# First loads of a two-block transformer kernel: smaller pieces in another order, and zero matmuls on TensorE ahead of the first GEMM

## The chip, the core and the metric

The kernel runs on one core of a Trainium2 chip. The metric is the device time of one execution in microseconds; a run has several executions, and the median is quoted. One further execution is recorded by the hardware profiler, and every row below comes from that one.

## The reference, cut to what matters

Two transformer blocks run one after the other on 256 tokens of width 1024, all in float32. What the change touches is the very beginning: the RMS norm and the first product of block one.

```python
h = _rmsnorm(x, g_mix[l])              # x: 256 x 1024
z = h @ w_in[l]                        # w_in: 1024 x 5632; q is columns 2048 to 3071
x_rnn, g_rnn, q, k, v, gate_a, gate_b = jnp.split(z, SPLIT_IDX, axis=-1)
...                                    # RG-LRU branch, sliding window attention, gates, w_out
x = x + jnp.square(jax.nn.relu(hm @ w_up[l])) @ w_down[l]
...                                    # gated embedding; then block two: latent attention, pooling,
                                       # memory attention, and a mixture of 32 experts, top 2
return rms_norm(h, final_norm_g)
```

The norm's factor is a number per token, so the kernel multiplies the raw x by the gain g_mix first, runs the product, and applies the factor to the result.

## The kernel before, in words

**Products.** TensorE multiplies in float32 by a split: each operand is written as a high part in the fast float32 format plus the rest, and a product is three matmuls, high by high (L313), low by high (L314) and high by low (L315). `split` (L278) makes the parts: ScalarE casts the high part (L279), VectorE subtracts it from the source (L280). This is done for the activations (tile `st`) and for every weight (tile `raw` into `w`).

**The first GEMM.** `gemm` (L317) takes two halves of the tokens (t = 0, 1), 512 output columns, and eight blocks of 128 rows of the weight (k = 0 to 7). The weight comes in raw tiles of four blocks (1 MB each), and each raw tile is split and used in *parts* of two blocks. So the first GEMM (the first 512 columns of q) is four parts of 12 matmuls each: part 0 has k = 0 and 1, part 1 has k = 2 and 3 (both from the first raw tile), parts 2 and 3 have k = 4 to 7 (from the second raw tile).

**The order.** `run` (L242) writes the program part by part. Ahead of a part it splits weights ahead: before part 0 the weights of parts 0 and 1; before part 1 those of parts 2 and 3; from then on always two parts ahead (L257: `ahead <= done + min(self.LEAD, done + 1)`, with LEAD = 2). A callback in `after_split[1]` runs between the split of part 0's weights and that of part 1's. After a part's matmuls the work that was put off with `later(n, fn)` comes due: `later(0)` after the first part, `later(1)` after the second, and so on. Then the background generators ("lanes") each go one step, or two while fewer than FAST = 18 parts are done (L272). From the beginning to `self.region.close` (due after the fourth part) the order on every engine is as written (`manual_schedule`); what is written later is ordered by a planner that may also put it into earlier gaps, until a second region in written order before the experts (L1054). The engines take their instructions strictly in the order they were given.

**The start.** `setup` (L498) loads the first quarter of x, loads two row tiles of small parameters, builds the identity, and turns the first of the row tiles into columns (gain vectors). `start` (L613) transposes x in quarters of 256 KB, (c, t) being the columns c·512 to c·512+511 of token half t: four transposes (L286), then a multiply by the gain on VectorE (L290, tile `xg`), then a split into `st`. Quarter (0,0) is transposed in `start`, quarter (0,1) in the callback, the quarters (1,0) and (1,1), which are k = 4 to 7, after part 0. `factor` computes the norm's factor after part 1. The loads on the queue of SyncE (SP) are: x (0,0); weight blocks k = 0, 1 (512 KB); x (0,1); weight blocks k = 2, 3 (512 KB); x (1,0); x (1,1); then raw tiles of 1 MB. The first four stand in `rawload` (L300).

**Later.** `background` lanes carry the attention (`swa_q`, `swa_k`) and the recurrence; `self.step(lambda: self.until(swa))` (L685) empties the attention lanes before the product that needs them. The experts at the end stream their weights from memory.

Of the kernel before, what the change touches and what calls it, by code (L numbers as in the profile page):

```python
# [12 lines left out]
BF16 = mybir.dt.bfloat16  # L13
# [8 lines left out]
P = 128  # L22
# [77 lines left out]
class Net:  # L100
# [199 lines left out]
    def rawload(self, w, k0, nk, c0, n):  # L300
        src = w[k0 * P:(k0 + nk) * P, c0:c0 + n].rearrange("(k p) n -> p k n", p=P)
        if not self.raws:
            def first(tile):
                self.nc.sync.dma_start(tile[:, 0:2, 0:n], src[:, 0:2])
                self.load_x(0, 1)
                self.nc.sync.dma_start(tile[:, 2:4, 0:n], src[:, 2:4])
                self.load_x(1, 0, 1)
            return Raw(first)
        return Raw(lambda tile: self.nc.sync.dma_start(tile[:, 0:nk, 0:n], src))
# [7 lines left out]
    def gemm(self, st, KT, w, c0, n, evac):  # L317

        accs = {}
        for k0 in range(0, KT, 4):  # L320
            nk4 = min(4, KT - k0)
            r = self.rawload(w, k0, nk4, c0, n)
            for q in range(0, nk4, 2):
                nk = min(2, nk4 - q)
                def fn(h, l, k=k0 + q, nk=nk):
# [172 lines left out]
    def setup(self):  # L498
        nc, a, cp = self.nc, self.a, self.cp
# [6 lines left out]
        nc.vector.memset(warm, 0.0)  # L506
        nc.scalar.activation(warm, warm, AF.Tanh)
        self.ident = cp.tile([P, P], F32, name="ident")
        make_identity(nc, self.ident)
# [7 lines left out]
        turn(0, 0, _SPLIT_ROW)  # L517
        self.later(1, lambda: turn(1, _SPLIT_ROW, N_ROW - _SPLIT_ROW))

    def load_x(self, c, *ts):  # L520
# [92 lines left out]
    def start(self):  # L613

        nc, st = self.nc, self.st0
        g = self.col("g_mix")
        part = lambda c, t: self.X[t][:, c * 512:(c + 1) * 512]
        x0 = self.trans_gain(part(0, 0), 0, 4, g)
        def first():
            self.split(x0, st.v(0, 0, 0, 4), st.v(1, 0, 0, 4))  # L620
            self.trans_split([(1, part(0, 1))], st, 0, 4, g)
        self.after_split[1] = first
        def factor():
# [6 lines left out]
            for t in range(2):  # L630
                st.r[t], st.rh[t] = r[:, t:t + 1], rh[:, t:t + 1]
        self.later(0, lambda: self.trans_split([(t, part(1, t)) for t in range(2)], st, 4, 4, g))
        self.later(1, factor)
        self.later(3, self.region.close)
        def more():
            self.setup1()
            self.lanes.insert(0, self.setup_steps())
        self.later(3, more)

# [1135 lines left out]
```

## Time and profile before

| | |
|---|---|
| median of 3 runs | 972.24 us (971.6 to 977.51) |
| the profiled execution | 971.25 us |
| its span, first to last instruction | 969.5 us |
| PE busy (matmuls) | 900.0 us, 93% of the span |
| DVE busy | 547.4 us, 56% |
| ACT busy | 472.6 us, 49% |
| moved by DMA | 222.65 MB |

The span is 1.75 us shorter than the time of the same execution; the rest lies before the first and after the last recorded instruction. PE is TensorE, PEld its weight loads, DVE VectorE, ACT ScalarE, POOL GpSimd, SP the engine that issues most DMAs; a "q" behind a name is the engine's sequencer, which issues DMAs and waits. All times in rows are microseconds from the start of the span. An arrow "<-" in brackets names what ended an engine's wait.

### The profile page before, as it was taken

How to read it: one execution, taken by the hardware profiler on the slowest of the kernel's cores; microseconds unless marked ns; L12 is line 12 of the kernel's file. 1: busy time of each engine (PE TensorE's matmuls, PEld its weight loads, DVE VectorE, ACT ScalarE, POOL GpSimd, SP SyncE). 2: the span in 40 equal slices, each digit the busy share in tenths (PEclk: the TensorE clock that was granted, in tenths of full speed). 3: DMA queues.
4: the chain of work that ended last, by engine and by line, in shares of the span. 5: the costliest groups of instructions: out<-in, count | busy, mean ns of one | idle time of the engine just before them, and what ended most of it. 6: DMA issues, size and time to landing. Idle time of an engine off the chain costs nothing.

```text
span 969.5 us, 14260 instructions
## 1 busy us (share of the span) xinstructions
PE 900.0 (93%) x5265; PEld 697.7 (72%) x5265; DVE 547.4 (56%) x1101; ACT 472.6 (49%) x900; POOL 34.6 (4%) x71
## 2 busy tenths in 40 slices
PE   6999999999999999999999999999989999647775
PEld 5889898888999999988888887998864444213112
DVE  5986889776675555577765568755455221101002
ACT  5666789654664544456666635545432323002002
POOL 4200000000000000000200000000000000000000
PEclk9999999999999999999999999999998999779868
DMA  9644235495375555544854544454848999999994
GB/s 292 217 153 153 88 131 177 140 321 176 108 247 185 202 178 190 178 145 145 259 180 153 188 150 161 164 184 138 307 166 322 403 405 406 402 406 410 375 408 174
DMA packets 97784, 222.65 MB, mean 230 GB/s; under 512 B 9378, under 2 KB 13739, under 8 KB 96427
## 3 DMA queue, kind: packets, MB, share of 16 engines
q1 hardware_dynamic: 94016, 218.91, 63.5%
q10 hardware_dynamic: 3691, 2.74, 0.9%
q8 instruction: 44, 0.72, 0.3%
q14 instruction: 33, 0.27, 0.1%
HBM read 220.59 MB, written 1.05 MB: 229 GB/s over the span
## 4 chain that ended last, share of the span: by engine, by line
PE 80%; DMA 13%; DVE 3%; issue 1%; ACT 1%; POOL 0%; SPq 0%; DVEq 0%; ACTq 0%; POOLq 0%
PE acc L313 18%; PE acc L315 18%; PE acc L314 17%; DMA raw<-in_w_exp_up_dram 6%; PE pt L1540 5%; PE pt L314 3%; PE pt L315 3%; PE pt L313 3%; DMA rawa<-in_w_exp_down_dram 3%; PE pt L1562 2%; PE pt L1490 1%; DMA rawa<-in_w_exp_up_dram 1%; PE pt L286 1%; DMA raw<-in_w_exp_gate_dram 1%; PE acc L1571 1%
## 5 line engine op out<-in xcount | busy, mean ns | idle before, releaser
L280 DVE TENSOR_TENSOR w<-raw,w 128x512 fp32r<-128x512 f32 (+4 forms) x288 | 273.6, 969 | 115.6 <-ACT w L279 113.6
L279 ACT CAST w<-raw 128x512 fp32r<-128x512 f32 (+4 forms) x288 | 236.3, 847 | 153.9 <-PE acc L315 117.0
L313 PE MATMUL acc<-w,st 128*128 128x512 f32 (+2 forms) x508 | 197.2, 392 | 0.0
L314 PE MATMUL acc<-w,st 128*128 128x512 f32 (+2 forms) x508 | 196.9, 388 | 0.0
L315 PE MATMUL acc<-w,st 128*128 128x512 f32 (+2 forms) x508 | 192.9, 388 | 0.2 <-DVE w L280 0.2
L1540 PE MATMUL pt<-raw,xg 128*32 128x512 f32 (+1 forms) x360 | 95.7, 669 | 40.3 <-DMA raw<-in_w_exp_up_dram 40.3
L315 PEld LDWEIGHTS acc<-w,st 128*128 128x128 f32 x508 | 95.5, 188 | 18.9 <-DVE w L280 0.6
L313 PEld LDWEIGHTS acc<-w,st 128*128 128x128 f32 x508 | 95.8, 189 | 18.4 <-ACT st L279 0.5
L314 PEld LDWEIGHTS acc<-w,st 128*128 128x128 f32 x508 | 95.7, 189 | 17.4 <-DVE st L280 0.2
L1540 PEld LDWEIGHTS pt<-raw,xg 128*32 128x32 f32 (+1 forms) x360 | 22.1, 126 | 95.1 <-issue 91.4
L280 DVE TENSOR_TENSOR y<-pt,y 128x512 fp32r<-128x512 f32 x20 | 13.8, 692 | 129.3 <-ACT y L279 129.3
L314 PE MATMUL pt<-st,w 128*128 128x256 f32 x256 | 72.4, 283 | 1.9 <-DVE w L280 1.9
L315 PE MATMUL acc<-st,w 128*128 128x256 f32 x256 | 73.7, 288 | 0.0
L313 PE MATMUL acc<-st,w 128*128 128x256 f32 x256 | 73.5, 287 | 0.0
L314 PE MATMUL acc<-st,w 128*128 128x256 f32 x256 | 73.4, 287 | 0.0
L313 PE MATMUL pt<-st,w 128*128 128x256 f32 x256 | 72.3, 283 | 0.0
L315 PE MATMUL pt<-st,w 128*128 128x256 f32 x256 | 71.8, 283 | 0.0
L1556 ACT COPY hT<-pt 128x256 f32<-128x256 f32 x10 | 3.7, 373 | 97.4 <-PE pt L1554 97.4
L314 PEld LDWEIGHTS pt<-st,w 128*128 128x128 f32 x256 | 49.1, 192 | 2.3 <-DVE w L280 2.1
L313 PE MATMUL acc<-w,hid 128*128 128x512 f32 x128 | 50.0, 390 | 0.0
L314 PE MATMUL acc<-w,hid 128*128 128x512 f32 x128 | 49.9, 390 | 0.0
L315 PE MATMUL acc<-w,hid 128*128 128x512 f32 x128 | 49.8, 389 | 0.0
(393 smaller groups left out, 1391.0 us busy)
## 6 DMA issues: line engine op xcount, KB each, us to landing
raw<-in_w_in_dram SPq DMA_DIRECT2D x31, 1024.0 KB, 5.3
raw<-in_w_exp_gate_dram SPq DMA_DIRECT2D x45, 512.0 KB, 9.5
raw<-in_w_exp_up_dram SPq DMA_DIRECT2D x45, 512.0 KB, 10.2
rawa<-in_w_exp_down_dram SPq DMA_DIRECT2D x44, 512.0 KB, 9.1
raw<-in_w_up_dram SPq DMA_DIRECT2D x16, 1024.0 KB, 5.7
raw<-in_w_down_dram SPq DMA_DIRECT2D x16, 1024.0 KB, 6.2
raw<-in_w_exp_down_dram SPq DMA_DIRECT2D x10, 1024.0 KB, 11.0
rawa<-in_w_exp_gate_dram SPq DMA_DIRECT2D x38, 256.0 KB, 7.8
```

Source lines behind the costliest of these rows:

```text
L279: self.nc.scalar.copy(h, src)
L280: self.nc.vector.tensor_sub(l, src, h.bitcast(F32))
L286: self.nc.tensor.transpose(p[:, i, :], src[:, i * P:(i + 1) * P], self.ident)
L313: mm(acc, xh, wh, start=start, stop=False)
L314: mm(acc, xl, wh, start=False, stop=False)
L315: mm(acc, xh, wl, start=False, stop=stop)
L1490: nc.tensor.matmul(p, xs[t][i][:, k * P:(k + 1) * P], oh[b, t], start=n == 0, stop=n == 3)
L1540: nc.tensor.matmul(guP[p][q].rearrange("s (j f) -> s j f", j=2), xg[b, hf][:, k, j * P + q.start:j * P + q.stop], gu_of(x, k), start=kt == ...
L1556: nc.scalar.copy(hT[p], q)
L1562: nc.tensor.matmul(q[s], hT[p][:, f, s], d_of(x, f, c), start=f == 0, stop=f == 1)
L1571: nc.tensor.matmul(acc[t, c], stt[b][:, j, t, :], y[p, c][i], start=False, stop=p == NP - 1 and i == 1)
```

## The change

The first raw tile is cut into parts of one, one and two blocks instead of two and two, so that the first GEMM has five parts. Its loads are cut in the same way, and x (0,1) is issued between the first and the second block. Both quarters (0,0) and (0,1) are now transposed in `start`, and the callback only splits them. A bf16 tile of zeros is set on VectorE, and TensorE multiplies it by itself into a PSUM tile that nobody reads: six matmuls of 512 columns in `setup`, one after the first group of transposes and four after the second. What was put off to after the first, second and fourth part is put off by one part more; the second row tile's transpose (`later(1)` in `setup`) is not.

```diff
@@ rawload, first raw tile
-                self.nc.sync.dma_start(tile[:, 0:2, 0:n], src[:, 0:2])
+                self.nc.sync.dma_start(tile[:, 0:1, 0:n], src[:, 0:1])
                 self.load_x(0, 1)
+                self.nc.sync.dma_start(tile[:, 1:2, 0:n], src[:, 1:2])
                 self.nc.sync.dma_start(tile[:, 2:4, 0:n], src[:, 2:4])
                 self.load_x(1, 0, 1)
@@ gemm
+            cuts = [0, 1, 2, 4] if not self.raws else [*range(0, nk4, 2), nk4]
             r = self.rawload(w, k0, nk4, c0, n)
-            for q in range(0, nk4, 2):
-                nk = min(2, nk4 - q)
+            for q, nk in zip(cuts, (b - a for a, b in zip(cuts, cuts[1:]))):
@@ setup
         nc.scalar.activation(warm, warm, AF.Tanh)
+        self.zeros = self.act([P, 512], BF16, name="zeros")
+        nc.vector.memset(self.zeros, 0.0)
+        self.unused = self.pt()
+        self.keep(6)
@@
+    def keep(self, n):
+        for _ in range(n):
+            self.nc.tensor.matmul(self.unused, self.zeros[:, 0:P], self.zeros, start=True, stop=True)
@@ start
-        x0 = self.trans_gain(part(0, 0), 0, 4, g)
+        xs = []
+        for t in range(2):
+            xs.append(self.trans_gain(part(0, t), 0, 4, g))
+            self.keep(1 + 3 * t)
         def first():
-            self.split(x0, st.v(0, 0, 0, 4), st.v(1, 0, 0, 4))
-            self.trans_split([(1, part(0, 1))], st, 0, 4, g)
+            for t in range(2):
+                self.split(xs[t], st.v(0, 0, t, 4), st.v(1, 0, t, 4))
...
-        self.later(0, lambda: self.trans_split([(t, part(1, t)) for t in range(2)], st, 4, 4, g))
-        self.later(1, factor)
-        self.later(3, self.region.close)
+        self.later(1, lambda: self.trans_split([(t, part(1, t)) for t in range(2)], st, 4, 4, g))
+        self.later(2, factor)
+        self.later(4, self.region.close)
...
-        self.later(3, more)
+        self.later(4, more)
```

## Rows read from the trace of the kernel before

**Rows 1.** The page: busy time by engine, and the chain that ended last by engine.
```profile
PE 900.0 (93%) x5265; PEld 697.7 (72%) x5265; DVE 547.4 (56%) x1101; ACT 472.6 (49%) x900; POOL 34.6 (4%) x71
PE 80%; DMA 13%; DVE 3%; issue 1%; ACT 1%; POOL 0%; SPq 0%; DVEq 0%; ACTq 0%; POOLq 0%
```

**Rows 2.** Waits, whole span: who waited for whom, total us, times, longest.
```profile
PE pt L1540 <- DMA raw<-in_w_exp_up_dram: 40.3, 16, 10.2
PE pt L286 <- DMA x<-in_x_dram: 3.9, 1, 3.9
...
PE pt L1321 <- DVE sel L1318: 2.6, 1, 2.6
...
SPq L1445 <- DVE w L280: 18.7, 3, 9.0
```

**Rows 3.** Chain of waits, 0 to 60 us: start, length, what.
```profile
1.75 6.84 DMA x<-in_x_dram
8.63 1.12 PE pt L286 x4
9.75 0.43 PE acc L313
...
13.35 0.23 PE acc L315
13.59 0.45 PE pt L286 x4
...
14.79 0.63 ACT st L279 x2
...
15.91 1.06 ACT w L279
16.99 1.24 DVE w L280
18.27 0.50 PE acc L315
```

**Rows 4.** Timeline, 0 to 20 us: start, length, engine, line, what.
```profile
0.89 0.06 DVE L506 MEMSET s<- 128x1 f32 x1 [0.89 <-PEq L1759]
1.27 0.43 SPq L304 DMA_DIRECT2D raw<-in_w_in_dram  x1
3.51 0.38 PE L515 MATMUL pt<-ident,rows 88*128 88x88 f32 x1 [3.51 <-DMA rows<-in_rows_dram]
4.80 0.69 DVE L290 TENSOR_TENSOR xg<-pt,cols 128x512 f32<-128x512 f32 x1 [0.24 <-PE pt L286]
5.31 0.33 SPq L523 DMA_DIRECT2D x<-in_x_dram  x1
5.68 0.69 SPq L309 DMA_DIRECT2D raw<-in_w_in_dram  x1
7.86 0.68 DVE L280 TENSOR_TENSOR st<-xg,st 128x512 fp32r<-128x512 f32 x1
19.27 0.20 DVE L516 COPY cols<-pt 128x49 f32<-128x49 f32 x1
```

**Rows 5.** First DMAs, issue to landing: L304, L523 (four issues), then the 1 MB tile.
```profile
DMA to landing us min/median/max: 4.3/4.3/4.3
...
DMA to landing us min/median/max: 2.8/6.8/7.3
...
raw<-in_w_in_dram SPq DMA_DIRECT2D x1, 1024.0 KB, 8.6
```

**Rows 6.** Windows: stretch, length, busy by engine (count), PEclk, DMA share, GB/s.
```profile
5.00:8.00 3.00, 0.00 (x0) 0.00 (x0) 1.78 (x3) 1.56 (x2) 0.00 (x0) 1.00 0.84 202
8.00:11.00 3.00, 2.37 (x8) 2.08 (x9) 1.23 (x2) 0.49 (x1) 1.62 (x9) 1.00 1.06 393
...
150.00:160.00 10.00, 10.00 (x49) 8.34 (x49) 9.85 (x16) 9.76 (x23) 0.00 (x0) 1.00 0.48 156
```

**Rows 7.** Line 848, the attention lanes' last product: idle time before it.
```profile
  ACT r L727: 2.4, 2
```

## The prediction

> **What bounds the kernel now.** I read the page first. The reader is to see that PE is busy 93% of the span and carries 80% of the chain, and that DMA carries most of the rest [rows 1]. The list of waits says where PE stands still: 40.3 us before the experts' products, for their weights, 3.9 us for x and 3.51 us for the parameter rows at the very start, and elsewhere in pieces of 2.6 us and less [rows 2, 4]. So from the first GEMM to the experts PE is a queue with hardly a gap, and a microsecond won or lost in the first 19 us arrives at the end as a microsecond. The experts' part is bound by DMA, but the load queue there waits for buffers that VectorE's splits set free (L1445 waits for L280, 18.7 us [rows 2]), and these follow PE, so it shifts along.
>
> Then the chain of the first stretch, which is the one that the change touches [rows 3]. It goes: x (0,1) lands 6.84 us after its issue at 1.75; its transposes; part 0's twelve matmuls, the first ones at 0.43 us each and the last at 0.23; transposes of k = 4 to 7; VectorE's gain multiply; ScalarE's cast of x; then ScalarE's cast and VectorE's subtraction of the weights of part 2, and its third matmul, which starts at 18.27 and, 0.50 later, ends at 18.77. From there PE runs without a gap. That end, 18.77, is the number to beat: it is matmul 27 of the GEMM. The granted clock's column shows 1.00 all along [rows 6], but 0.43 us for 512 columns is the level of 1.2 GHz and 0.23 that of 2.4, so the first half dozen matmuls run at the lower one.
>
> **The change, part by part.** *Zero matmuls in setup.* VectorE sets the zeros right after its first memset, which it did at 0.89 [rows 4], so PE can start at some 1.3 us. Six matmuls at 0.43 are 2.6 us and end near 4.0. The first row transpose stood at 3.51 [rows 4]: it and the first x transposes come 0.5 us later, and the gain multiply, 4.80 to 5.49 before [rows 4], ends near 6.0. Nobody needs it before the second quarter.
>
> *Order of the loads.* x (0,1) now has 512 KB ahead of it on SP's queue instead of 768. The weight piece that had that place landed 4.3 us after its issue at 1.27, at 5.6 [rows 4, 5]. So x (0,1) lands at 5.6 instead of 8.6; the bounds are these two, and I take 5.6 because the bytes ahead are the same. Block k = 1 gets the old place of x (0,1), 8.6. Four transposes (1.12) and a gain multiply (0.69) bring the second quarter to 7.4. The five further zero matmuls on PE cost 0.43 and 1.7 us at the lower clock, up to 8.4; they are hidden, because VectorE is later than that: its subtractions now queue behind the second multiply, w (half the size, 0.68) to 8.1, x (0,0) to 8.8, x (0,1) to 9.5, and w of k = 1 to 10.2 [rows 4].
>
> *First matmuls.* The first can start at 8.4, the second at 8.8, and the twelve of parts 0 and 1 end near 11.3 if the clock is up (12 by 0.23 is 2.8 us); before, twelve had ended at 13.6 [rows 3]. That is 2.3 us won, of which 6 by 0.20, 1.2 us, is the clock. If this came through, the kernel would be 2.3 us faster.
>
> *What is late next.* Behind part 1 stand the transposes of k = 4 to 7. Quarter (1,1) is loaded by the last of four issues that took 6.8 to 7.3 us [rows 5], the last issued at 5.31 [rows 4]: it is there between 12.1 and 12.6, whatever PE does. So PE waits, transposes until 13.1 (0.45), and runs part 2 (k = 2, 3; 2.8 us) to 15.8. In itself that is still fine.
>
> *The moved step.* The x work for k = 4 to 7 was due after part 0, ahead of the split of the second raw tile. Now it is due after part 1; and before part 1 `run` splits two parts ahead, which are k = 2, 3 and k = 4, 5. The weights k = 4, 5 are in the second raw tile. So on ScalarE and VectorE, which keep the written order here, the x work now stands **behind a weight split that waits for the second raw tile**. That tile was issued at 5.68 [rows 4] and landed 8.6 us later [rows 5], at 14.3. The sum from there: ScalarE's cast 1.06, to 15.4; VectorE's subtraction 1.24, to 16.6; the second row tile's copy, which is now also due here, 0.20 [rows 4], to 16.8; gain multiply 0.69, to 17.5; ScalarE's cast of x 0.63, to 18.1; VectorE's second multiply ends then too; its subtraction 0.68, to 18.8. Then the second and third matmul of k = 4 end at 19.1 and 19.35. Before it was 18.77. **The head is 0.6 us longer, not 2.3 shorter**: the gain is spent in PE's wait for k = 4 to 7, from 15.8 to 18.
>
> Bounds for the unknown landing of the second raw tile: its bytes ahead are the same, so I take 14.3. Earlier: from 5 to 8 us DMA moved 202 GB/s, from 8 to 11 us 393 [rows 6]; if the new order closed that, 1.46 us (3 by 191/393), the head would be 0.9 us shorter. Later: one load more stands in the queue. 256 KB took 2.8 us and 512 KB 4.3 [rows 5], so two halves one after the other cost 2 by 2.8 less 4.3, 1.3 us more: the head would be 1.9 us longer. I take no extra, because DMA overlaps several loads and is full from 8 us on, at a share of 1.06 [rows 6].
>
> The Trainium skill speaks against the cut: its page "DMA: Bandwidth & Descriptors", section Bandwidth, tells one to batch transfers to a megabyte or more, and its anatomy section gives each DMA (on the path issued by GpSimd) a fixed part of about 2.0 us beside its bytes. By that figure, as an estimate, one piece more would cost up to 2.0 us if nothing overlapped, and the sum would be near 974.8. The trace agrees that a piece has a fixed part (half the bytes took 2.8 us, not 2.15 [rows 5]), but not that the parts add up while other loads are under way.
>
> *The rest.* One part more before the eighteenth means that the lanes make one step fewer while they step twice. It costs nothing as long as they are empty when `until` asks; see the second rival. The profiled execution would come to 971.25 + 0.6 = 971.9; the median of the runs stands 1.0 us above that execution, so I say 972.24 + 0.6 = **972.8**.
>
> **Rivals.** *A: the gain comes through.* The second raw tile and quarter (1,1) land early enough, or x's casts are ordered ahead of the waiting weight split. For it: DMA has room between 5 and 8 us. Against: the bytes and the written order. Time: 972.24 − 2.3 = 969.9.
>
> *B: slower, by the attention lanes.* They lose a step, and the last product of attention (L848) is emitted in the drain ahead of the product that needs it. ScalarE and VectorE are almost full there (9.76 and 9.85 of 10 us [rows 6]), so a late step is not caught up. That line has PE and its weight loads waiting 2.4 us in all for ScalarE already [rows 7]; as much again gives 972.8 + 2.4 = 975.2. It decides if the lanes are not empty when `until` is reached. Against: over the span they are busy 56 and 49% [rows 1], so the planner has room elsewhere.
>
> *C: the zeros don't lift the clock.* Then the first twelve matmuls end at 12.5 instead of 11.3, still no later than quarter (1,1) lands: 972.8 again, and A shrinks to 971.1. The trace before has no matmul of zeros, so nothing decides it; transposes alone, at 8.63, did not spare the first matmuls the 0.43 [rows 3]. It lies across the others; 1 in 5.
>
> **How the numbers follow.** Forecast (head −0.9 to +1.9) 0.47, A 0.27, B 0.19, and 0.07 for a planner that orders the later work otherwise by over 1% of the time, 9.7 us, which is about what a measurement can tell from no change. For that much PE has no gaps ahead of the experts to win, and to lose it a whole stage would have to fall out of step: 0.03 faster, 0.04 slower. The range goes from A with a microsecond of spread (968.8) to B with the late bound (974.1 + 2.4) and a microsecond (977.5): the median of three also moves, one run before was at 977.51. All three named cases lie within 1%: 0.93.
>
> **What would show it.** In the changed kernel's trace: x (0,1)'s transposes near 6 us; twelve matmuls done by 11 to 12.5; the first real matmuls at 0.23 (A, forecast) or 0.43 (C); VectorE idle before the subtraction of k = 4, 5 for ScalarE, and ScalarE for the second raw tile's DMA, near 14.3; PE idle for VectorE's `st` or `xg` near 16 to 18; matmul 27 ending near 19.35. If it ends at 17 or less the step on the moved work is wrong. B would show as a longer wait at L848 near 170 us. If the difference of the two times isn't that of matmul 27, the carry-through is wrong.

## The result, and the profile after

The changed kernel takes 986.0 us (median of 4 runs, 984.92 to 986.32), beside 971.92 for the kernel before (4 runs, 971.36 to 977.51): a ratio of 1.0136, with a 95% interval of 1.0115 to 1.0156. (The ratios here and below are estimated from all the runs, and need not be the quotients of the two medians.) It is 14 us slower; 972.8 was forecast, and the range ended at 977.5. The profiled execution took 985.95 us, with a span of 984.3; before it was 971.25 and 969.5. The difference of the spans, 14.8 us, is what has to be found. Lines below the edit have moved: L313 to L315 are now L314 to L316, L726 is L740, L727 is L741, L848 is L862.

First the page, busy time by engine and the chain by engine, as in [rows 1].

```profile
PE 910.6 (93%) x5276; PEld 700.6 (71%) x5276; DVE 546.5 (56%) x1103; ACT 473.1 (48%) x901; POOL 35.9 (4%) x71
PE 79%; DMA 14%; DVE 3%; ACT 2%; issue 1%; SPq 0%; POOL 0%; ACTq 0%; DVEq 0%; POOLq 0%
```

The shares tell nothing: PE is busy 10.6 us longer, with 11 instructions more, the eleven zero matmuls. A busy PE can be a slow PE. VectorE and ScalarE are busy for as long as before, to within a microsecond. Nor does the list of waits over the whole span show it: the experts' wait for their weights is 40.4 us, as it was [rows 2].

```profile
PE pt L1554 <- DMA raw<-in_w_exp_up_dram: 40.4, 16, 10.0
```

So I looked for landmarks: the same instruction in both traces. Two do it: the first eviction of the branch gates (ScalarE), and the first multiply that takes the attention's projection (VectorE, tile `gate`). Timeline of the kernel before (columns: start, length, engine, line, what):

```profile
69.57 1.86 ACT L430 ACTIVATE gate<-acc,s 128x512 f32<-128x512 f32 x3
...
181.40 1.28 DVE L414 SCALAR_TENSOR_TENSOR gate<-gate,acc 128x512 f32<-128x512 f32 x2
```

The same two in the changed kernel:

```profile
71.51 1.85 ACT L431 ACTIVATE gate<-acc,s 128x512 f32<-128x512 f32 x3
...
195.60 0.68 DVE L415 SCALAR_TENSOR_TENSOR gate<-gate,acc 128x512 f32<-128x512 f32 x1
```

At the first the changed kernel is 1.9 us behind, at the second 14.2, at the end 14.8. So between these two executions the head makes 1.9 us, and **12.3 us are lost between 70 and 196 us**, in a stretch that the change does not touch. The head isn't the same in every execution, as the part on the prediction shows; the 12.3 are counted from landmark to landmark and don't hang on it.

**The head.** The chain of waits from 0 to 60 us, which answers to [rows 3] (start, length, what):

```profile
5.64 3.78 DMA x<-in_x_dram
9.44 0.75 DVE w L280
10.19 0.67 DVE st L280
10.90 0.79 PE acc L315
...
15.53 0.43 PE acc L316
15.96 0.27 PE pt L520
16.23 1.06 PE pt L286 x8
17.30 0.23 PE acc L314
```

Its first line is a later quarter of x; the profile infers that link, and VectorE stood in its multiply for x (0,1) until 9.5. From the second on, the matmuls of parts 0 and 1 follow each other at 0.43 us, from 10.90 to 15.96, in spite of the zeros. The timeline shows how that came (it answers to [rows 4]; what is in brackets is the idle time before, and who ended it):

```profile
1.30 2.74 PE L529 MATMUL pt<-zeros 128*128 128x512 bf16 x6 [1.30 <-DVE zeros L510]
...
8.14 0.66 PE L286 MATMUL pt<-ident,x 128*128 128x128 f32 x4 [2.67 <-DMA x<-in_x_dram]
8.31 8.05 SPq L310 DMA_DIRECT2D raw<-in_w_in_dram  x4
...
8.63 1.09 PE L529 MATMUL pt<-zeros 128*128 128x512 bf16 x4
...
14.41 1.05 ACT L279 CAST w<-raw 128x1024 fp32r<-128x1024 f32 x1 [2.76 <-DMA raw<-in_w_in_dram]
...
15.49 1.23 DVE L280 TENSOR_TENSOR w<-raw,w 128x1024 fp32r<-128x1024 f32 x1 [2.13 <-ACT w L279]
...
16.63 0.20 DVE L521 COPY cols<-pt 128x49 f32<-128x49 f32 x1
16.90 1.29 DVE L290 TENSOR_TENSOR xg<-pt,cols 128x512 f32<-128x512 f32 x2
17.62 1.22 ACT L279 CAST st<-xg 128x512 fp32r<-128x512 f32 x2 [2.17 <-DVE xg L290]
```

After the six zeros and the first transposes PE waits 2.67 us for x (0,1), which lands at 8.14. The second transposes run fast (4 in 0.66, where [rows 3] has 1.12), and so do the four zeros (1.09 for 4). Then the clock falls, as the windows show (stretch, length, PE, PEld, DVE, ACT and POOL busy, PEclk, DMA share, GB/s):

```profile
5.00:9.00 4.00, 1.33 (x8) 0.68 (x7) 0.86 (x2) 1.24 (x2) 0.59 (x4) 1.00 0.90 284
9.00:9.50 0.50, 0.50 (x5) 0.29 (x2) 0.50 (x2) 0.00 (x0) 0.41 (x3) 0.96 0.97 340
9.50:16.00 6.50, 5.75 (x14) 3.58 (x12) 4.37 (x7) 3.13 (x4) 6.50 (x16) 0.50 1.03 364
```

In the landings (least, median, most), which answer to [rows 5], the first 256 KB of weights took 3.7 us and the slowest quarter of x, (0,1), 6.4:

```profile
DMA to landing us min/median/max: 3.7/3.7/3.7
...
DMA to landing us min/median/max: 2.8/6.1/6.4
```

This is one execution. The same beginning ran again in e1, e9, e10, e11, e13 and e14 below. There too PE waits 2.84 to 2.90 us for x (0,1), but the transposes behind the wait take between 0.66 and 1.12 us, fewer matmuls run at 0.43 us, and the twelfth ends between 14.1 and 15.2 us.

**The stretch that is lost.** Windows of the kernel before, then of the changed kernel, of the attention and the recurrence; they carry [rows 6] on.

```profile
60.00:160.00 100.00, 98.92 (x719) 88.69 (x718) 82.35 (x204) 78.47 (x197) 0.27 (x1) 1.00 0.39 130
160.00:180.00 20.00, 20.00 (x101) 16.07 (x100) 13.37 (x26) 16.91 (x33) 0.00 (x0) 1.00 0.47 157
```

```profile
60.00:160.00 100.00, 100.00 (x717) 88.94 (x716) 77.19 (x194) 71.55 (x178) 1.11 (x1) 1.00 0.39 134
160.00:170.00 10.00, 6.69 (x33) 4.75 (x31) 6.53 (x8) 8.71 (x12) 0.00 (x0) 0.99 0.51 180
170.00:180.00 10.00, 5.68 (x14) 3.41 (x15) 9.31 (x26) 8.52 (x28) 0.00 (x0) 0.50 0.00 0
180.00:190.00 10.00, 10.00 (x41) 7.70 (x40) 2.43 (x3) 6.88 (x13) 0.00 (x0) 0.82 0.00 0
```

The reader is to see three things. PE is busy without a break to 160 us and then idle for 7.6 of 20 us. From 170 us on it runs at half the clock for 10 us. And ScalarE (the fourth figure) and VectorE (the third) did 6.9 and 5.2 us less work by 160 us than in the kernel before, though PE did as much (717 matmuls to 719): their work is *late*; over the whole span it is not more. From 60 to 200 us PE's busy time is 6.55 us less (132.37 to 138.92); the lower clock costs 10 by 0.18 in the last row and 5.68 by 0.50 in the one above, 4.6 us. Together 11.2 of the 12.3.

What PE waits for there (timeline, PE alone):

```profile
164.91 0.39 PE L316 MATMUL acc<-w,st 128*128 128x512 f32 x1
167.46 0.70 PE L740 MATMUL pt<-xc,w_ig 128*128 128x256 f32 x2 [2.17 <-ACT r L741]
...
176.51 1.08 PE L472 MATMUL pt<-ident,pr 128*128 128x128 f32 x4 [3.01 <-DVE pr L464]
...
180.72 0.78 PE L314 MATMUL acc<-w,st 128*128 128x512 f32 x1
```

Between 164.91 and 180.72 PE gets no matmul of a GEMM. In its order stand the recurrence's gates (L740) and the transposes of the attention's probabilities (L472), and both wait for ScalarE's and VectorE's attention work. The 2.4 us of wait for `r` ahead of the attention's last product that [rows 7] shows, where the prediction had looked for trouble, are gone (0.4 us and less for each releaser); it is the products ahead of it that wait.

The attention's exponentials come in four batches on ScalarE (L452 before, L453 after). The fourth begins at 156.11 before and 169.87 after; the second at 100.19 and 109.38; the first, less the head's 1.9, at the same time. So the delay begins between the first and the second batch. That is where the lanes stop stepping twice: after 18 parts, which the new, smaller parts let come one part earlier in the work. Counted in the written program, batches one to four stand behind parts 16, 20, 25 and 30 in the kernel before; in the changed kernel the first is in the same place of the work, and the others are one part later. A part takes 5 to 6 us here (five parts lie between batches two and three, 25.9 us, and between three and four, 30.1). Less the head, the second batch is 7.3 us late and the fourth 11.8, so more is lost than the place in the program.

### The profile page after: what moved, and what is told of

It reads as the page before. It is cut to its first block, busy times and chain, and to the rows that moved or that the text cites. A ratio compares the mean times of both kernels' runs of the same rounds, so it can differ in the third digit from the quotient of the medians.

```text
span 984.3 us, 14287 instructions
## 1 busy us (share of the span) xinstructions
PE 910.6 (93%) x5276; PEld 700.6 (71%) x5276; DVE 546.5 (56%) x1103; ACT 473.1 (48%) x901; POOL 35.9 (4%) x71
## 3 DMA queue, kind: packets, MB, share of 16 engines
q10 hardware_dynamic: 3691, 2.74, 0.9%
## 4 chain that ended last, share of the span: by engine, by line
PE 79%; DMA 14%; DVE 3%; ACT 2%; issue 1%; SPq 0%; POOL 0%; ACTq 0%; DVEq 0%; POOLq 0%
PE acc L316 17%; PE acc L315 17%; PE acc L314 17%; DMA raw<-in_w_exp_up_dram 5%; PE pt L1554 5%; DMA rawa<-in_w_exp_down_dram 3%; PE pt L315 3%; PE pt L316 3%; PE pt L314 3%; PE pt L1576 2%; DMA rawa<-in_w_exp_up_dram 2%; DMA raw<-in_w_exp_down_dram 1%; PE pt L286 1%; PE pt L1504 1%; DVE w L280 1%
## 5 line engine op out<-in xcount | busy, mean ns | idle before, releaser
L280 DVE TENSOR_TENSOR w<-raw,w 128x1024 fp32r<-128x1024 f32 (+3 forms) x289 | 273.9, 965 | 122.5 <-ACT w L279 120.7
L279 ACT CAST w<-raw 128x1024 fp32r<-128x1024 f32 (+3 forms) x289 | 236.5, 844 | 167.6 <-PE acc L316 123.0
L315 PE MATMUL acc<-w,st 128*128 128x512 f32 (+2 forms) x508 | 198.6, 392 | 0.8 <-DVE st L280 0.8
L314 PE MATMUL acc<-w,st 128*128 128x512 f32 (+2 forms) x508 | 198.4, 393 | 0.0
L316 PE MATMUL acc<-w,st 128*128 128x512 f32 (+2 forms) x508 | 194.0, 390 | 0.0
L1554 PE MATMUL pt<-raw,xg 128*32 128x512 f32 (+1 forms) x360 | 95.1, 682 | 40.4 <-DMA raw<-in_w_exp_up_dram 40.4
L315 PEld LDWEIGHTS acc<-w,st 128*128 128x128 f32 x508 | 96.3, 190 | 18.9 <-DVE st L280 1.6
L316 PEld LDWEIGHTS acc<-w,st 128*128 128x128 f32 x508 | 96.1, 190 | 19.0 <-issue 1.1
L314 PEld LDWEIGHTS acc<-w,st 128*128 128x128 f32 x508 | 96.2, 190 | 18.7 <-issue 0.6
L315 PE MATMUL pt<-st,w 128*128 128x256 f32 x256 | 72.4, 283 | 1.8 <-DVE w L280 1.8
L316 PE MATMUL acc<-st,w 128*128 128x256 f32 x256 | 73.1, 286 | 0.0
L315 PE MATMUL acc<-st,w 128*128 128x256 f32 x256 | 73.1, 286 | 0.0
L314 PE MATMUL acc<-st,w 128*128 128x256 f32 x256 | 73.0, 286 | 0.0
L314 PE MATMUL pt<-st,w 128*128 128x256 f32 x256 | 72.3, 283 | 0.0
L316 PE MATMUL pt<-st,w 128*128 128x256 f32 x256 | 71.8, 283 | 0.0
L315 PEld LDWEIGHTS pt<-st,w 128*128 128x128 f32 x256 | 49.1, 192 | 2.2 <-DVE w L280 2.0
L357 POOL TENSOR_TENSOR s<-s,mhalf 128x1 f32<-128x1 f32 (+3 forms) x21 | 20.3, 970 | 823.8 <-DVE s L355 807.8
L314 PE MATMUL acc<-w,hid 128*128 128x512 f32 x128 | 50.0, 390 | 0.0
L315 PE MATMUL acc<-w,hid 128*128 128x512 f32 x128 | 49.9, 390 | 0.0
## 6 DMA issues: line engine op xcount, KB each, us to landing
raw<-in_w_exp_down_dram SPq DMA_DIRECT2D x10, 1024.0 KB, 10.6
```

Source lines behind the costliest of these rows:

```text
L279: self.nc.scalar.copy(h, src)
L280: self.nc.vector.tensor_sub(l, src, h.bitcast(F32))
L314: mm(acc, xh, wh, start=start, stop=False)
L315: mm(acc, xl, wh, start=False, stop=False)
L316: mm(acc, xh, wl, start=False, stop=stop)
L357: self.nc.gpsimd.tensor_tensor(r, ms, self.mhalf[:, 0:w], op=ALU.pow)
```

## The experiments

Each was timed in five rounds beside the kernel before on the same chip; ratios have 95% intervals. The first theory: the lanes lose one step, because FAST counts parts and there is one part more. Its rival: the head, or the other order that a planner finds for it. A second question was whether zeros lift the clock at all, and a third whether the moved step that the prediction described is there.

**e1: the changed kernel with the step given back.**

```diff
-    FAST = 18
+    FAST = 19
```

> The changed kernel with FAST = 19 instead of 18, so that the background lanes get as many double steps per unit of work as before the change. Theory L (the 12.3 us between 70 and 196 us come from the lanes' one lost step): that stage is as long as before, and the time is 986.0 - 12.3 = 973.7 us; what stays is the head, whose 27th matmul ends near 20.8 instead of 18.77. Rival P (the planner orders the later work otherwise because the region in written order closes later, or the late head upsets it): the stage stays 12 us longer, and the time stays at 986.

973.63 us beside 973.21, ratio 1.0003 (0.9992 to 1.0013). Batches two and four of the exponentials begin at 102.4 and 158.3, some 2.2 us after those of the kernel before, which is the head; from 160 to 180 us PE has no gap:

```profile
160.00:180.00 20.00, 20.00 (x101) 16.08 (x100) 14.39 (x29) 16.97 (x36) 0.00 (x0) 1.00 0.48 158
```

One number takes back all of the loss that can be measured.

**e2: the kernel before with a step taken away.**

```diff
-    FAST = 18
+    FAST = 17
```

> The kernel before with FAST = 17 instead of 18 and nothing else: one double step less, the head untouched. Theory L: 972.0 + 12.3 = 984.3 us, with PE idle and the lower clock between 160 and 185 us as in the changed kernel. Rival P: 972, within a microsecond.

983.83 us beside 973.21, ratio 1.011 (1.0089 to 1.013). The head is that of the kernel before (first eviction of the gates at 69.8), and the loss is there without one line of the change: batches two and four at 107.7 and 168.2, and the window reads

```profile
160.00:180.00 20.00, 12.95 (x51) 9.21 (x51) 14.52 (x32) 17.65 (x42) 0.00 (x0) 0.74 0.18 59
```

The lost step is shown as the cause, from both sides.

**e3: the changed kernel with FAST = 19 and no zeros.** All `keep` calls and the tile of zeros are taken out.

```diff
-        self.zeros = self.act([P, 512], BF16, name="zeros")
-        nc.vector.memset(self.zeros, 0.0)
-        self.unused = self.pt()
-        self.keep(6)
...
-            self.keep(1 + 3 * t)
```

> As the first, with the eleven matmuls of zeros and their tile taken out; loads and order stay as changed. Theory C (the zeros raise the clock, the wait for x of 2.7 us lets it fall again just as the GEMM begins, and so all twelve first matmuls run at 0.43 us): without zeros the clock rises during the first matmuls as before the change, the 27th ends near 19.4 (the second raw tile behind the moved step then sets it), and the time is 972.6 us. Rival (the zeros cost nothing, the cut loads do): the 27th ends near 20.8 as with zeros, 973.7 us.

974.63 us, ratio 1.0018 (1.0007 to 1.003). Matmul 27 starts at 21.1, later than the 20.6 of e1 and than expected: here the second raw tile lands 7.8 us after its issue at 8.47, at 16.3; in e1 it took 7.2 from 8.53, to 15.7. Taking the zeros out wins nothing, so they are not what costs.

**e4: the same with more zeros,** so that PE's wait for x (0,1) is filled.

```diff
-            self.keep(1 + 3 * t)
+            self.keep(12 - 8 * t)
```

> As the first, with twelve matmuls of zeros instead of one after the first group of transposes, enough to fill PE's wait for the second quarter of x. Theory C: the clock doesn't fall, the first twelve matmuls take 0.23 us each, and the 27th ends near 19.4, held by the moved step behind the second raw tile's landing near 14.4; the time is 972.6 us. Rival (the clock falls whatever is done, or zeros don't count): twelve at 0.43 us again, the 27th near 20.8, 973.7 us. If the moved step doesn't hold, the 27th ends near 17.5 and the time is 970.7.

972.94 us, ratio 1.0001 (0.9987 to 1.0015). The granted clock is 1.00 from 5 to 20 us, and the first twelve matmuls, from the second on, follow at 0.23 us. And now the moved step shows (timeline, PE, ScalarE and VectorE):

```profile
16.73 1.05 ACT L279 CAST w<-raw 128x1024 fp32r<-128x1024 f32 x1 [4.96 <-DMA raw<-in_w_in_dram]
...
19.08 1.28 DVE L290 TENSOR_TENSOR xg<-pt,cols 128x512 f32<-128x512 f32 x2
19.79 1.22 ACT L279 CAST st<-xg 128x512 fp32r<-128x512 f32 x2 [2.01 <-DVE xg L290]
...
20.46 0.50 PE L314 MATMUL acc<-w,st 128*128 128x512 f32 x1 [2.83 <-ACT st L279]
```

PE, fast now, waits 2.83 us for an x that stands behind the cast of a weight that waits 4.96 us for its DMA. Matmul 27 starts at 21.53: what the clock gave is spent in this wait. Behind it the clock falls once more (0.52 from 22 to 24 us). The trace shows the mechanism and not its usual price, for the profiled execution was the slowest of twelve, 978.13 us.

**e5: e4 with the split of part 3 written one part later,** so that the x work for k = 4 to 7 stands ahead of it (L257).

```diff
-                while ahead < len(parts) and ahead <= done + min(self.LEAD, done + 1):
+                while ahead < len(parts) and ahead <= done + min(self.LEAD, max(1, done)):
```

> As the fourth (FAST = 19, wait filled with zeros), and the weights of part 3 (k = 4, 5) are split one part later, so that the x work for k = 4 to 7 stands ahead of that split on ScalarE and VectorE again. Theory M (the moved step behind the second raw tile is what holds the 25th matmul, 2.83 us of PE idle for ScalarE's cast of x in the fourth run): that wait is gone, and the 27th matmul then waits for its weights only, the raw tile's landing (15.8 to 16.7 in the runs so far) and 1.05 + 1.23 us: it ends near 18.6 to 19.4 instead of 21.9. Time 972.9 - 2.7 = 970.2 us. Rival (the late landing alone holds it): the 27th ends at 21 or later, 972.9 us.

972.34 us beside 972.38, ratio 1.0001 (0.9992 to 1.0011). The wait is gone:

```profile
15.18 1.22 ACT L279 CAST st<-xg 128x512 fp32r<-128x512 f32 x2 [3.58 <-DVE xg L290]
...
16.30 2.00 ACT L279 CAST w<-raw 128x1024 fp32r<-128x1024 f32 x2
...
17.45 0.46 PE L314 MATMUL acc<-w,st 128*128 128x512 f32 x1
```

Matmul 25 starts at 17.45 instead of 20.46, matmul 27 at 18.67 instead of 21.53. But only a part of these 2.9 us is the order's. The second raw tile was issued at 9.06 in e4 and took 7.7 us, to 16.7; in e5 it was issued at 8.29 and took 6.0, to 14.3. With e4's order and that landing, matmul 27 would start 4.8 us behind the cast, as in e4, at 19.1. So by this estimate some 0.4 us are the order, and the rest is when the tile comes. The wait itself is what the order removes: x no longer hangs on that tile. The gain of 2.7 us that was expected is not in the times; e5's trace is that of its fastest execution, 971.08 us, and e4's that of its slowest.

**e6: the kernel before with zeros alone,** six in `setup` and 14 after the first group of transposes; loads, cuts and lanes as before.

```diff
+        self.keep(6)
...
+        self.keep(14)
```

> The kernel before, loads, parts and FAST as they were, with six matmuls of zeros in the setup and fourteen after the first group of transposes, which fill PE's wait for x (0,1). Theory C (the clock stays up over a filled wait): the first six matmuls at 0.23 instead of 0.43 us, part 0 ends 1.2 us earlier, the 27th matmul ends near 17.8 instead of 18.9, and the time is 972.1 us where the kernel before has 973.2. Rival (the loads set the head, the clock is hidden): the 27th ends at 18.8 as before, 973.2 us.

971.46 us beside 972.38, ratio 0.9995 (0.9985 to 1.0004). The clock is 1.00 throughout, the first matmuls run at 0.23, matmul 27 starts at 17.82 instead of 18.27 [rows 3]. It is the best of all that ran, but its interval holds 1.

**e7: the same with six zeros and one,** so that the wait stays open.

```diff
+        self.keep(6)
...
+        self.keep(1)
```

> The kernel before with the change's zeros alone, six in the setup and one after the first transposes, the wait for x (0,1) left open. Theory C: the clock is raised by the zeros and falls in or after the open wait of 3 us, so that between six and twelve of the first matmuls run at 0.43 us; the 27th ends between 18.8 and 20.0, the time is 973.2 to 974.4 us. Rival (zeros alone help): the 27th ends near 17.8, 972.1 us.

972.52 us, ratio 1.0002 (0.999 to 1.0014). PE waits 3.54 us for x (0,1) until 9.01, and then (windows):

```profile
9.00:10.00 1.00, 0.99 (x5) 0.99 (x6) 0.03 (x1) 0.00 (x0) 0.41 (x3) 0.63 1.08 401
10.00:12.00 2.00, 2.00 (x6) 1.51 (x6) 1.32 (x2) 1.30 (x2) 2.00 (x9) 0.50 1.05 393
```

Zeros lift the clock (e4, e6); here it is down again behind an open wait of 3.5 us.

**e8: the kernel before with a step more.**

```diff
-    FAST = 18
+    FAST = 19
```

> The kernel before with FAST = 19 instead of 18: one double step more. Theory L1 (what counts is that the attention lanes are done in time): a step more doesn't hurt, 973.2 us or up to 1.1 less, the one wait before L848. Rival L2 (18 is one lucky order, and any shift costs): PE idle between 100 and 190 us again, several us more, up to 984.

976.33 us beside 972.38, ratio 1.0046 (1.003 to 1.0062). A step more isn't better, against the first expectation: the fourth batch comes sooner, at 151.8, and PE still loses 3.6 us from 160 to 180 (1.8 each for a gate multiply of VectorE at L313 and for the gate's tanh on ScalarE at L726). Sooner isn't safer; 18 parts of the old cut is a fit.

The second theory was about how the lost step costs 12 us. In the written order of the changed kernel the recurrence's gate comes between the scores of the fourth batch and its exponentials, and both take PSUM tiles of the same four.

**e9, e10, e11: the changed kernel with the gate one part later; with its PSUM tile from the accumulators; one part sooner** (L742, L739, L742).

```diff
-            self.later(2, gate)
+            self.later(3, gate)
```

```diff
-                    p = self.pt()[:, 0:S]
+                    p = self.accp()[:, 0:S]
```

```diff
-            self.later(2, gate)
+            self.later(1, gate)
```

> The changed kernel with one number altered: the recurrence's gate products come due three parts after their block instead of two (L742). The lanes keep the lost step. Theory S (the loss between 70 and 196 us comes from the gate product being written between the scores and the exponentials of the attention's last group, with three of the four transposing PSUM tiles held by scores and ScalarE's function table changing in between): one part later the gate is written behind the exponentials, TensorE's waits at L740 and L472 of some 7 us vanish, TensorE is busy over 9 of 10 us from 160 to 180, and the time is 974 to 977. Rival T (the lost lane step itself costs, by later attention results): the gate's place doesn't matter, 985 to 987. Against S too: later gates could make the recurrence late, since it has a part less; then the first L740 waits go and others come.

> The changed kernel with the gate product's PSUM tile taken from the four accumulators of the GEMM instead of the four transposing tiles that it shares with the scores (L740). Written order and lanes as in the changed kernel. If the shared PSUM tiles are what ties the gate to the attention's exponentials (theory S, its PSUM half): TensorE's wait at L740 for ScalarE goes from 2.8 us to under 0.5 in the stretch from 160 to 180 us, and the time falls by 3 to 10 us, to 976 to 983. If it is only ScalarE's order (gate, table, then exponentials) or the lost lane step: the wait at L472 for the probabilities stays at 4 us and the time at 985 to 987. An accumulator taken by the gate can also make a GEMM block wait, which would show as waits at L314 for VectorE or ScalarE.

> The changed kernel with the gate products due one part after their block instead of two (L742). They are then written ahead of the scores of the last group, not between scores and exponentials. The lanes keep the lost step. Theory S: the collision is gone, 974 to 978, and no wait of over 1 us at L740 or L472 between 150 and 190 us. Rival T (the lost lane step itself): 985 to 987.

982.66 (1.0106; 1.009 to 1.0122), 979.21 (1.0074; 1.0053 to 1.0094) and 983.95 us (1.0124; 1.0107 to 1.014), beside 972.38. **The theory's half on the written order falls**, by e9: with the gate behind the exponentials some 3 us of 13 are recovered, by the ratios, where 9 to 12 were expected. The wait only changes its name: PE stands 5.4 us at L740 for the exponentials (L453). e11 does not test it, against what was written ahead of it: one part sooner, the gate of the next block comes to stand between the fourth batch's scores and exponentials, in the program as in the trace (the last score at 162.7 us, a gate at 162.8, the first exponential at 170.4). **The half on the PSUM tiles came out as expected**: in e10 the wait at L740 is gone, there is no gap from 160 to 180 us, and the time lies in the range of 976 to 983. But more has changed than that wait. With the step still lost, the second batch begins at 96.3 and the fourth at 143.0, earlier than in the kernel before, and PE now loses 3.5 us and some clock between 80 and 100:

```profile
80.00:100.00 20.00, 16.48 (x116) 13.50 (x115) 15.53 (x47) 13.84 (x49) 0.00 (x0) 0.91 0.00 1
...
160.00:180.00 20.00, 20.00 (x89) 16.54 (x90) 17.30 (x23) 15.80 (x24) 0.00 (x0) 1.00 0.58 183
```

So how late the lost step makes the batches hangs on the PSUM tiles too, and that is a part of what the planner has to order by.

**e12: the kernel before with the gate one part sooner** (L728), which puts it between scores and exponentials with all lane steps kept.

```diff
-            self.later(2, gate)
+            self.later(1, gate)
```

> The kernel before, with the gate products due one part after their block instead of two (L728). The lanes keep all their steps, but the gate is now written between the scores and the exponentials of the last group, as in the changed kernel. Theory S: the loss appears without any lost lane step: waits at L726 and L471 of 3 us and more between 140 and 180 us, and a time of 977 to 985. Rival T (the lost lane step itself): nothing is lost, 971 to 973.

975.35 us, ratio 1.004 (1.0021 to 1.0059): 3.0 us, which is below what was expected, with waits of 1.3 us and less, and PE idle for 0.9 us from 160 to 180. The gate's place is a part of it and not the main one.

The third theory: what costs is that the attention's last batch is late, so that PE comes to the products that hang on it with nothing else in its order. Its rival: the order that the missing step gives early on.

**e13, e14: the changed kernel with the step given back later,** after 22 parts and after 27.

```diff
-            for _ in range(1 + (done < self.FAST)):
+            for _ in range(1 + (done < self.FAST or done == 22)):
```

> The changed kernel, FAST 18, with the lost lane step given back later: the lanes step twice once more after part 23 (done == 22 when the loop of run looks at it), ahead of the attention's third group. Theory U (what costs is when the attention's last groups get done): the second group's exponentials stay late (near 109 us as in the changed kernel), those of the third and fourth come back to near 128 and 158, TensorE is busy over 9 of 10 us from 160 to 180, and the time is 973 to 977. Rival V (what costs is the order that the missing step gives early, from the second group on): 983 to 987.

> The changed kernel, FAST 18, with the lost lane step given back later still, when 27 parts are done, between the third and the fourth group of the attention. Theory U: second and third group late (near 109 and 140 us), the fourth back to near 158 to 162; 973 to 979. Rival V: 983 to 987. If the third group's lateness is what costs, it is as slow as the changed kernel although the fourth group is early.

981.4 (1.0098; 1.0076 to 1.0119) and 985.16 us (1.013; 1.0108 to 1.0151), beside 972.22. Both expectations of the theory were missed, and in the same way: the steps did not bring the fourth batch back to 158, but to 164.1 and 169.1. e14 is in the rival's range and e13 1.6 us below it. A step given back late does not make up for the early one, though in e13 it puts the third and fourth batches back to the place in the program that they have in the kernel before.

**e15, e16, e17: the kernel before with one, two and four steps left out late,** at 23 parts, at 26 and 28, and at 25 to 28.

```diff
-            for _ in range(1 + (done < self.FAST)):
+            for _ in range(1 + (done < self.FAST) - (done in (26, 28))):
```

> The kernel before, FAST 18, with one lane step left out when 23 parts are done, so that the first groups of the attention are as in the kernel before and the later ones lose a step. Theory U: the second group's exponentials at 100 us as before, the fourth's at 165 or later, TensorE short of work between 160 and 180 us, and 981 to 985. Rival V (the early step): 971 to 974.

> The kernel before, FAST 18, with two lane steps left out late, when 26 and 28 parts are done; second and third group of the attention as before (100 and 126 us). Theory U (the lateness of the last group is what costs, once TensorE has no other work to cover it): the fourth group's exponentials at 161 to 168, TensorE short of work after 160 us, and 976 to 984 by the relation of the earlier runs. Rival V (the early step, which sets the second group, is what costs): 971 to 975 wherever the fourth group lies.

> The kernel before, FAST 18, with four lane steps left out late, when 25 to 28 parts are done. Theory U: second group at 100 us as before, the fourth later than 168, waits of TensorE as in the changed kernel (several us at L471 and L726 between 155 and 185 us) and 983 to 992. Rival V: 971 to 976.

975.37 (1.0019; 1.0005 to 1.0032) beside 972.22, and 978.81 (1.0064; 1.0052 to 1.0076) and 981.23 us (1.0087; 1.0074 to 1.01) beside 972.53. In all three the second batch is in time (100.8 to 101.6); only later ones are late. In e15 both expectations were missed: the fourth batch begins at 158.6, not 165, and the time is above the rival's range. ScalarE's first exponential of batches two and four in e16, and PE's window:

```profile
101.14 0.36 ACT L452 ACTIVATE pr<-pt,s 128x128 f32<-128x128 f32 x1
...
164.50 0.35 ACT L452 ACTIVATE pr<-pt,s 128x128 f32<-128x128 f32 x1
...
160.00:180.00 20.00, 17.31 (x72) 13.13 (x71) 12.56 (x31) 17.80 (x43) 0.00 (x0) 0.91 0.30 104
```

So a late last batch costs some 6 us by itself: in e16 the third is in time too (127.0, beside 126.1), and where the steps are left out only the attention's lanes are under way. In e17 the third batch is 8 us late as well, and it is 8.5 us; 983 to 992 was expected, and it stayed 2 us below that.

The runs that differ in lanes or gates in one table, by their ratio (e3 to e7 differ in the head only). Busy and clock are PE's from 160 to 180 us; the start of the batches is not corrected for the head.

| kernel | batch 2 | batch 4 | PE busy of 20 | clock | ratio |
|---|---|---|---|---|---|
| before | 100.2 | 156.1 | 20.0 | 1.00 | 1 |
| e1 changed, step back | 102.4 | 158.3 | 20.0 | 1.00 | 1.0003 |
| e15 before, one left out late | 100.8 | 158.6 | 19.6 | 1.00 | 1.0019 |
| e12 before, gate sooner | 100.7 | 160.2 | 19.1 | 1.00 | 1.0040 |
| e8 before, a step more | 100.5 | 151.8 | 16.4 | 1.00 | 1.0046 |
| e16 before, two left out late | 101.1 | 164.5 | 17.3 | 0.91 | 1.0064 |
| e10 changed, gate's PSUM tile | 96.3 | 143.0 | 20.0 | 1.00 | 1.0074 |
| e17 before, four left out late | 101.6 | 169.1 | 15.7 | 0.83 | 1.0087 |
| e13 changed, back after 22 | 110.7 | 164.1 | 15.1 | 0.74 | 1.0098 |
| e9 changed, gate later | 110.6 | 168.1 | 13.3 | 0.74 | 1.0106 |
| e2 before, a step less | 107.7 | 168.2 | 13.0 | 0.74 | 1.0110 |
| e11 changed, gate sooner | 108.4 | 170.4 | 12.1 | 0.72 | 1.0124 |
| e14 changed, back after 27 | 108.7 | 169.1 | 11.4 | 0.77 | 1.0130 |
| changed | 109.4 | 169.9 | 12.4 | 0.75 | 1.0136 |

What PE stands idle there, and the clock that falls with it, goes with the time in the main. The exceptions are e8, which idles at full clock, and e10, which doesn't idle there at all and loses its time between 80 and 100. With the fourth batch at the same time (e17 and e14, 169.1) and the head too (first eviction of the gates at 71.0 and 70.8), a late second batch goes with 4 us more. e2 loses its step ahead of the second batch and e15 behind it, and both then have the third and fourth in the same places of the program; these begin at 138.3 and 168.2 in e2, but at 127.3 and 158.6 in e15. So most of the lateness is settled by the second batch, which is nearer to what the rival says.

**What stays open:** why one lane step early in the stretch moves the second batch by 7.5 us (e2) and the fourth by 12, why both come early in e10 with the step still lost, and why the planner leaves GEMM matmuls behind the waiting products. All of it lies in the planner's costs and in the order that it finds, which no run takes apart. Nor is it settled why e8 pays.

## Why the prediction was wrong

- **"The rest"**: this is the step that failed. The lost lane step was seen, and was put at nothing "as long as they are empty when `until` asks". Counting the steps in the written program, they are empty there in the kernel before and in the changed one, so the condition held, and it cost 12.3 us all the same (10.7 in e2, where nothing else is changed). Whether the lanes are empty before the product that needs them is not what counts; in the runs of the table it is, in the main, when the last batch of the attention reaches ScalarE, against the point at which PE has nothing else in its order.
- **Rival B** had the direction, the place (near 170 us) and the reason (a late step isn't caught up where ScalarE and VectorE are full [rows 6]). Its price was taken from the wait at one line [rows 7], 2.4 us, in which TensorE's own wait is only 1.1 and the rest its weight loads'; the runs show 10 to 12. It left out the wait of every product that hangs on the batch, and the clock, which falls while PE waits (4.6 of the 12.3). And "over the span they are busy 56 and 49%" was no argument against: the average says nothing about 160 to 180 us, where ScalarE had 17.2 of 20 (16.9 in the kernel before).
- **Carry-through**: "a whole stage would have to fall out of step" had 0.04. That is what happened. The prediction's own sign for it, a difference that isn't that of matmul 27, is there: 2 us at matmul 27, 14.8 at the end. Where the order behind the head was kept, the carry-through held: in e1 and e3 to e7 the head differs from that of the kernel before by −0.4 to +4.8 us at the first eviction of the gates, and the attention's projection by the same to within 0.1 us.
- **Zeros in setup**: right. 1.30 to 4.04 (forecast 1.3 to 4.0), the row transpose at 3.84.
- **Order of the loads**: wrong. x (0,1) landed at 8.14, not 5.6: it did not get the landing of the weight piece that had stood in its place [rows 5]. "The bytes ahead are the same" was a misreading, too: that piece had 256 KB ahead of it, and only the sum with its own 512 KB is the same. The landing lies near the upper bound, 8.6. The first real matmul came at 9.31 instead of 8.4, the second at 10.90 instead of 8.8.
- **First matmuls, rival C**: twelve ended at 16.0, forecast 11.3. In the six other executions of this beginning they ended between 14.1 and 15.2. The zeros did lift the clock, as e4 and e6 show, but the late x left a wait, and the clock was down again for a part of the matmuls or all. C's wording, that they do not lift it, is not it either.
- **The moved step**: the mechanism is right. Its five instructions in a row, from the second raw tile's cast to that of x, began at 14.41, 15.49, 16.63, 16.90 and 17.62; the forecast had 14.3, 15.4, 16.6, 16.8 and 17.5. (The tile was issued at 8.31 and not at 5.68, and took 6.1 us and not 8.6; that the landing agrees is partly luck.) In the changed kernel PE, at half the clock, is later than that and does not wait for it; in e4 it is the limit, 2.83 us of wait, and in e5, where x stands ahead, PE waits for no x. Its size at the forecast's landing, estimated from e4 and e5, is about 0.4 us; a late landing makes it larger.
- **The head**: forecast +0.6, measured +1.9 at the first eviction of the gates, between two executions. That it meets the upper bound (+1.9) is luck: that bound was for a second raw tile landing late, and here it landed in time and the matmuls were slow. Over more executions the head varies by over a microsecond: that eviction comes at 69.6 to 71.0 us in seven with the old beginning (before, e2, e8, e12, e15 to e17) and at 70.5 to 71.8 in seven with the new one (changed, e1, e9, e10, e11, e13, e14), on average 0.9 later. So the forecast's size was about right, and by luck, for x (0,1) was late and the first matmuls slow, and PE waited for the moved step by 0.9 us at most in these seven, not 2. In the times a microsecond of head can't be seen: e1 and e4, whose profiled executions have heads 2.2 and 4.8 us longer, stand at 1.0003 and 1.0001, with intervals of a microsecond and more to each side.
- **The Trainium skill's rule** that speaks against small transfers ("DMA: Bandwidth & Descriptors", the fixed part of each DMA in its section "Anatomy of one DMA") would, as an estimate, have put the second raw tile up to 2 us later. The traces agree in part. With the new loads it landed between 14.3 and 14.7 us in six executions (14.4 in the changed kernel, 14.3 in e5), but at 15.5, 15.7, 16.3 and 16.7 in e10, e1, e3 and e4; with the old ones in nine executions (before, e2, e6 to e8, e12, e15 to e17) always between 14.2 and 14.8. So up to 2 us are there in some executions and nothing in most; that it is the fixed part of the added load is not shown.

## What to carry to other kernels

Where a schedule counts its own units (parts, tiles, steps), a new cut of the work changes every count behind it, hundreds of microseconds away: look for each constant that is compared with such a counter, and scale it. The price of a late background step isn't the wait of one line, but what the main engine has left in its order when it gets there; read it from the stage's window, with the clock that falls in the gap. One profile is one execution: before a microsecond of it is explained, see how far the same rows lie apart in others. And before a clock is warmed up, see that no wait follows behind which it is down again.

## What the runs showed of the hardware

- Where TensorE's granted clock falls is not fixed by the instructions. In seven executions with the same beginning PE waited 2.67 to 2.90 us for x (0,1). In the changed kernel and e1 the four transposes behind the wait took 0.66 us, and the clock fell about a microsecond after the wait; in the changed kernel it then stood at 0.50 from 9.5 to 16 us, though PE was busy for 5.75 of these 6.5, in e1 from 9.5 to 12.5. In e9, e10 and e11 the transposes took 0.82 to 1.02 us, and the clock is 0.50 from 9.0 to 9.5. "TensorE: Matmul & The Clock Gate" of the Trainium skill, in its section "HAM oscillation", describes waits for a DMA that make the work behind them start at the lower clock; e9, e10 and e11 agree, but in the changed kernel and e1 the first transposes behind the wait still ran at the higher one.
- The column of the granted clock does not show a cold start: it reads 1.00 at 1 to 4 us, where the six zeros took 2.74 us, 0.46 each, which is the level of 1.2 GHz. In e13 it reads 1.00 from 9.0 to 13.5 us as well, where matmuls follow each other at 0.43 us; there the transposes behind the wait took 1.12 us, so it isn't seen whether the zeros had lifted the clock at all.
- From 170 to 180 us, with PE idle for 4.3 of the 10 us, the clock stood at 0.50 as well; in e8, which idles 3.6 of 20 us in two pieces of 1.8, it stayed at 1.00.
